# Scores leave PSUM in segments of up to 1024 keys, and outputs share one bank, in a streaming encoder layer

## The chip, the cores and the metric

The kernel runs on one core of one Trainium2 chip. The metric is device time in microseconds (us), less is better. Engines: PE is TensorE (matmul, with PEld its weight loads), DVE is VectorE, ACT is ScalarE, POOL is GpSimd, and SP issues the DMAs. PSUM is where matmuls write; the kernel divides it into eight banks, each of 512 float32 columns on 128 partitions.

## The reference

One layer of an encoder is computed for a prompt of 2048 rows and for eight sampled streams of 16 new rows with 512 cached keys. Two attention branches run side by side: differential attention (four heads, each with two softmax components) and stick-breaking attention (eight heads).

```python
s = einsum('bqhcd,bkhcd->bhcqk', q, k) * 64 ** -0.5
p = softmax(where(mask, s, -inf), axis=-1)
w = p[:, :, 0] - lam * p[:, :, 1]                       # differential attention
...
z = einsum('bqhd,bkhd->bhqk', q, k) * 64 ** -0.5
log_1m = where(mask, log_sigmoid(-z), 0.0)
log_a = log_sigmoid(z) + cumsum(log_1m, axis=3, reverse=True) - log_1m
a = where(mask, exp(log_a), 0.0)                        # stick-breaking attention
...
ya = (rms_norm(oa) * silu(za)) @ w_branch_a
yb = (ob * silu(zb)) @ w_branch_b
y = x + gate * ((sigmoid(ga) * ya + sigmoid(gb) * yb) @ w_out)
```

The outputs are the normed `y` for prompt and sample, and the new keys and values of both branches.

## The kernel before

The program has three phases. In the first the rows are normed, modulated, transposed and written to DRAM as two float16 halves; the projection of the first rows begins there. The second, where most of the time goes, runs over eight units (`u` 0 to 7). An even unit (`kind` 0) is one differential head, an odd one (`kind` 1) two stick-breaking heads. Each unit takes the sample tile and then sixteen query tiles `t` of 128 rows. The third phase does the branch and output products of all tiles and, beside them, the sample's attention over its cache.

A step of the second phase for tile `t` mixes three streams: projections of later tiles (`project`, L428 for queries, keys, values; L504 for the gates; L517 and L521 transpose queries and keys), the scores of tile `t` (`scores`, L625), and the product of weights and values (`pv`, L703) of the tile two steps before (`PV_LAG` 2).

Scores are made in chunks of up to 512 keys. `chunk` (L632) takes one bank by `bank("s")`, runs two matmuls (L639, L640: queries are split into two halves) and, on the diagonal, a third one that adds the mask (L643). `evacuate` (L549) then reads the bank. In an even unit DVE scales it into the tile `sc_p` or `sc_n` and keeps the row maximum (L558). In an odd unit ACT writes the sigmoid into `sc_p` and the sigmoid of the negated score back into the bank (both by the helper at L119), and DVE runs a product scan over that bank into `sc_n` (`stick`, L616), from the last key to the first.

Two chunks make a segment of up to 1024 keys (`SEG` is 8 blocks of 128). For a whole segment `softmax_pair` or `stick_weights` (POOL, L622) makes the weights, `turn` splits them into float16 halves (L572 on ACT, L573 on DVE) and a DMA transposes them into `wt` (L580). `pv_block` multiplies them with the values into an output tile from `bank("o")` (L696 to L698 even, L700 and L701 odd), and `natural` reads it (L675 on ACT in an even unit, L680 on ACT and L681 on DVE in an odd one).

`BANKS` (L185) shares out the eight banks: two for projections (`mm`), three for scores (`s`), one for transposes and gates (`t`), two for outputs (`o`). They lie in one pool for the whole program. In the third phase the sample takes a bank `s` for the scores against its own new keys (L761), and for each of four pairs of streams a bank `t` for the product with cached values (L803), which ACT reads at once (`ot`, L806).

The code gives the program order, by costs in `interleave`. When the program is built, a scheduler reorders each engine's instructions along a simulated timeline, and adds the waits. An engine then runs its own in that fixed order. A tile of PSUM is taken again when all that used it are done; within one tile the waits go by bank, not by column.

Of the kernel before, what the change touches and what calls it, by code (L numbers as in the profile page):

```python
# [25 lines left out]
P = 128  # L26
# [83 lines left out]
def layer_kernel(ctx: ExitStack, tc: tile.TileContext, a: dict):  # L110
# [73 lines left out]

    BANKS = {"mm": 2, "s": 3, "t": 1, "o": 2}  # L185

    def bank(tag, dt=F32):
        return ps.tile([P, 512 if dt == F32 else 1024], dt, tag=tag, name=f"ps_{tag}", bufs=BANKS[tag])

# [435 lines left out]
    def scores(U, t, jobs):  # L625

        sc, kind = U["sc"], U["kind"]
        nch = t // 4 + 1
        own = [new_job(U, t, c, t + 1) for c in range(1 + kind)]
        jobs += own  # L630

        def chunk(c, ch):  # L632
            job = own[c if kind == 1 else 0]
            seg = job["segs"][ch * 4 // SEG]
            n = 512 if ch < t // 4 else (t % 4 + 1) * P
            p = bank("s")
            qst, kk = U["q", t], U["k"][ch]
            diag = ch == t // 4
            T.matmul(p[:, 0:n], qst[:, c, :], kk[:, c, 0:n], start=True, stop=False)  # L639
            T.matmul(p[:, 0:n], qst[:, 2 + c, :], kk[:, c, 0:n], start=False, stop=not diag)  # L640
            if diag:
                m = mask_a if kind == 0 else mask_b
                T.matmul(p[:, n - m.shape[1] : n], idb, m, start=False, stop=True)  # L643
            evacuate(job, seg, c, p, ch * 512 - seg["lo"] * P, n, sc[:, 3:4], sc[:, 4:5], ch)
            if kind == 0:
                if diag and c == 1:
                    softmax_pair(job)
                return
            i = job["segs"].index(seg)
            later = job["segs"][i + 1] if i + 1 < len(job["segs"]) else None  # L650
            stick(seg, later, ch * 512 - seg["lo"] * P, n, p)
            if ch * 4 == seg["lo"]:
                if later is not None:
                    stick_weights(job, later, None)
                if i == 0:
                    stick_weights(job, seg, later)
# [8 lines left out]
        order = [(c, ch) for ch in range(nch) for c in range(2)] if kind == 0 else \  # L665
                [(c, ch) for c in range(2) for ch in reversed(range(nch))]
        return ([(0.1, silu)] if kind == 1 else []) + [(2.0 if ch < t // 4 else (t % 4 + 1) / 2, lambda c=c, ch=ch: chunk(c, ch)) for c, ch in order]

# [34 lines left out]
    def pv(job):  # L703
# [18 lines left out]
    def sample(U, dec, qpad, cs):  # L722
# [33 lines left out]
        def scores_all():  # L756
# [33 lines left out]
        def output_cached(i):  # L790

            if i == 0:
                box["ot"] = dec.tile([P, P], F32, tag="ot", name="ot")
            vs = box.pop(("v", i))
            po = bank("t")
            for b in range(2):
                cols = slice((2 * i + b) * NS, (2 * i + b + 1) * NS)
                for c, job in enumerate(box["jobs"]):
                    r = slice(c * 64, c * 64 + 64) if kind == 1 else slice(0, P)
                    n = 0  # L800
                    for vf, wf in ((0, 0), (0, 1), (1, 0)):
                        for j in range(4):
                            T.matmul(po[r, cols], vs[:, b * 4 + j, vf, r], job["segs"][0]["wt"][:, wf * 5 + j, cols], start=(n == 0), stop=(n == 11))  # L803
                            n += 1
            c = slice(i * 32, i * 32 + 32)
            S.activation(out=box["ot"][:, c], in_=po[:, c], func=AF.Identity, scale=box["f"][:, 2:3])  # L806

# [103 lines left out]
    ab = con.tile([P, 2, KT, 9], F32, name="ab")  # L911
    with tc.tile_pool(name="p0", bufs=1) as p0:
        first_x = [free.pop() for _ in range(4)]
# [159 lines left out]
        def modulated(g):  # L1073
# [5 lines left out]
            def piece(k):  # L1079
# [3 lines left out]
                hp = box["hp"]  # L1083
                pt = bank("so"[k % 2])
                for i in range(nt):
# [56 lines left out]
    scp, wtp = (c01.enter_context(tc.tile_pool(name=n, bufs=1, reuse_waits="tile")) for n in ("scp", "wtp"))  # L1142
    (gts,) = buffers_of_4k("gt", 1)
    szs = wtp.tile([P, 4, P], F32, name="szs")
    rings = [szs[:, i, :] for i in range(4)] + [gts[:, i * P : (i + 1) * P] for i in range(4, 8)]
# [15 lines left out]
    def transposed(x16, dst, half):  # L1161

        pt = bank("s", F16)
        for k in range(KT):
            T.transpose(pt[:, k * P : (k + 1) * P], x16[:, half, k * P : (k + 1) * P], id16)  # L1165
        S.copy(out=dst[:, half * KT : (half + 1) * KT, :], in_=pt.rearrange("p (k n) -> p k n", n=P))  # L1166
# [260 lines left out]
```

## Time and profile before

| what | value |
|---|---|
| median of three runs | 2345.88 us (2344.93 to 2349.84) |
| the profiled execution, its own time | 2338.96 us |
| its span, first to last instruction | 2337.1 us |
| mean granted TensorE clock | 0.965 |
| PE, DVE, ACT, POOL busy | 2121.6, 1707.5, 1663.1, 661.3 us |
| DMA | 445.35 MB, 191 GB/s mean |

The profile shows one execution. Rows by shape read: line, engine, operation, what it writes and reads with shapes, count, then busy time, mean ns of one, and the idle time of the engine just before with what ended it. A row of waits reads: who waited for whom, total us, times, longest. Matmuls are pipelined, so a busy PE is not PE at its peak.

### The profile page before, as it was taken

The page shows a single profiled execution, that of the slowest core. Times are in us where ns is not written, and L with a number is a line of the kernel's source. Part 1 is how long each engine was busy: PE and PEld are TensorE (multiplying, and loading weights), DVE is VectorE, ACT ScalarE, POOL GpSimd, SP SyncE. Part 2 cuts the span into 40 slices and gives each one's busy share as a digit, 9 for nine tenths or more (in the row PEclk, how much of TensorE's full clock was granted, in tenths as well). Part 3 has the DMA queues.
Part 4 walks back from the last instruction along what each step waited for, and adds up shares of the span by engine and source line. Part 5 has one row for each costly group of instructions (what it writes and reads, how often), then busy time and mean ns, then how long its engine had stood idle before and what let it go on. Part 6 is the DMA issues. An engine that isn't in the chain of part 4 may idle for free. (4 is left out here: it accounts for less than half of the span.)

```text
span 2337.1 us, 42708 instructions
## 1 busy us (share of the span) xinstructions
PE 2121.6 (91%) x15272; PEld 1144.0 (49%) x15272; DVE 1707.5 (73%) x3653; ACT 1663.1 (71%) x3292; POOL 661.3 (28%) x578
## 2 busy tenths in 40 slices
PE   5998898998989899899999979999995878989998
PEld 3654454545545445445545545554553444544443
DVE  4658765779875677978667797777788777777663
ACT  4968777787877778778677777866777656756541
POOL 1222022356300334731024474103345111121111
PEclk7999999999999999999999999999997988999999
DMA  9777659897895898867577777756677999999521
GB/s 333 275 214 180 152 118 272 179 193 168 212 210 126 216 204 192 179 178 192 134 191 176 185 168 186 195 146 150 146 171 166 285 254 233 257 245 236 155 98 53
DMA packets 834358, 445.35 MB, mean 191 GB/s; under 512 B 537210, under 2 KB 777130, under 8 KB 833632
## 3 DMA queue, kind: packets, MB, share of 16 engines
q1 hardware_dynamic: 833196, 442.24, 76.0%
q8 instruction: 119, 1.95, 0.4%
q14 instruction: 95, 0.78, 0.1%
q10 hardware_dynamic: 948, 0.39, 0.1%
HBM read 245.60 MB, written 69.24 MB: 135 GB/s over the span
## 5 line engine op out<-in xcount | busy, mean ns | idle before, releaser
L622 POOL TENSOR_TENSOR sc_p<-sc_p,sc_n 128x127 f32<-128x127 f32 (+7 forms) x192 | 313.8, 1638 | 826.5 <-DVE sc_n L616 812.2
L428 PE MATMUL ps_mm<-wb,hs 128*128 128x512 f16 x1632 | 414.5, 382 | 1.5 <-DMA hs<-hT_d 1.3
L428 PEld LDWEIGHTS <-hs 128*128 128x128 f16 x3120 | 274.4, 98 | 257.3 <-DMA hs<-hT_d 11.8
L428 PE MATMUL ps_mm<-wa,hs 128*128 128x512 f16 x1488 | 374.6, 382 | 9.8 <-DVE qbuf L463 6.4
L616 DVE TENSOR_TENSOR_SCAN sc_n<-ps_s,sc_n,zero_t 128x512 f32<-128x512 f32 x192 | 245.4, 1278 | 68.4 <-ACT ps_s L119 65.0
L639 PE MATMUL ps_s<-k,qst 128*128 128x512 f16 (+3 forms) x640 | 224.2, 351 | 37.9 <-DVE sc_n L616 29.9
L573 DVE TENSOR_TENSOR sc_n<-sc_p,sc_n 128x128 f16<-128x128 f32 (+7 forms) x192 | 212.7, 1112 | 58.1 <-ACT sc_n L572 57.6
L504 PEld LDWEIGHTS <-hs 128*128 128x128 f16 x1632 | 156.6, 98 | 188.3 <-ACT qst L532 6.2
L119 ACT ACTIVATE sc_p<-ps_s,usc 128x512 f32<-128x512 f32 (+3 forms) x320 | 204.8, 640 | 30.2 <-PE ps_s L640 25.3
L640 PE MATMUL ps_s<-k,qst 128*128 128x512 f16 (+3 forms) x640 | 224.2, 352 | 0.0
L572 ACT CAST sc_n<-sc_p 128x128 f16<-128x128 f32 (+7 forms) x192 | 155.5, 813 | 78.5 <-POOL sc_p L622 76.9
L700 PE MATMUL ps_o<-v,wt 128*128 128x128 f16 x1088 | 171.5, 225 | 32.6 <-DMA wt<-sc_n 32.2
L119 ACT ACTIVATE ps_s<-ps_s,usc 128x512 f32<-128x512 f32 (+3 forms) x328 | 200.0, 610 | 0.0
L504 PE MATMUL ps_t<-wa,hs 128*128 128x512 f16 x816 | 192.9, 383 | 7.6 <-ACT qst L532 6.0
L504 PE MATMUL ps_t<-wb,hs 128*128 128x512 f16 x816 | 191.9, 380 | 1.2 <-DVE qst L532 0.8
L1344 PE MATMUL ps_o<-wo,wb 128*128 128x512 f16 x816 | 186.5, 383 | 4.1 <-ACT wb L1166 4.1
L701 PE MATMUL ps_o<-v,wt 128*128 128x64 f16 x1088 | 157.9, 197 | 0.0
L700 PEld LDWEIGHTS <-wt 128*128 128x128 f16 x1088 | 105.1, 101 | 98.1 <-DMA wt<-sc_n 45.1
L558 DVE TENSOR_SCALAR_CACHE_REDUCE sc_p<-ps_s,usc 128x512 f32<-128x512 f32 (+3 forms) x160 | 106.3, 665 | 42.4 <-PE ps_s L640 31.7
L616 DVE TENSOR_TENSOR_SCAN sc_n<-ps_s,zero_t 128x128 f32<-128x128 f32 (+3 forms) x128 | 104.1, 814 | 44.0 <-ACT ps_s L119 43.4
L558 DVE TENSOR_SCALAR_CACHE_REDUCE sc_n<-ps_s,usc 128x512 f32<-128x512 f32 (+3 forms) x160 | 106.3, 665 | 36.9 <-PE ps_s L640 26.3
L701 PEld LDWEIGHTS <-wt 128*128 128x128 f16 x1088 | 103.1, 100 | 54.3 <-issue 1.1
(360 smaller groups left out, 4493.6 us busy)
## 6 DMA issues: line engine op xcount, KB each, us to landing
hs<-hT_d SPq DMA_DIRECT2D x130, 512.0 KB, 4.2
g_d<-gt SPq DMA_DIRECT2D x68, 256.0 KB, 4.2
wb<-g_d SPq DMA_DIRECT2D x26, 512.0 KB, 4.8
out_dram<-pr SPq DMA_DIRECT2D x204, 64.0 KB, 2.3
o_d<-o SPq DMA_DIRECT2D x136, 64.0 KB, 2.2
hs<-o_d SPq DMA_DIRECT2D x17, 512.0 KB, 5.6
out_dram<-x SPq DMA_DIRECT2D x17, 512.0 KB, 2.8
wide<-in_w_ada_dram SPq DMA_DIRECT2D x8, 1024.0 KB
```

Of the source, the lines that this page charges most:

```text
L119: i = S.activation(**kw)
L428: T.matmul(box["p"], box["h"][:, hi, k, :], U["w"][k][:, wi, :], start=(n == 0), stop=(n == 3 * KT - 1))
L504: T.matmul(box["g"][:, 0:gw], box["h"][:, hi, k, :], U["wg"][k // per][:, k % per, wi, :], start=(j == 0), stop=(j == 3 * KT - 1))
L558: V.tensor_scalar(out=dst[:, lo : lo + n], in0=p[:, 0:n], scalar1=sc_pos, scalar2=None, op0=ALU.mult, op1=ALU.max, accum_out=job["mx"][:, ...
L573: V.tensor_tensor(out=lo, in0=src, in1=hi, op=ALU.subtract)
L616: V.tensor_tensor_scan(out=dst[:, lo : lo + n][:, ::-1], data0=src[:, 0:n][:, ::-1], data1=zero_t[:, 0:1].to_broadcast([P, n]), initial=fi ...
L622: G.tensor_tensor(out=p[:, 0:m], in0=p[:, 0:m], in1=n[:, 1 : m + 1], op=ALU.mult)
L639: T.matmul(p[:, 0:n], qst[:, c, :], kk[:, c, 0:n], start=True, stop=False)
L640: T.matmul(p[:, 0:n], qst[:, 2 + c, :], kk[:, c, 0:n], start=False, stop=not diag)
L700: T.matmul(po[:, c * P : (c + 1) * P], wt[:, wj, :], vt[:, c, :, :], start=first, stop=False)
L701: T.matmul(po[:, c * P : c * P + 64], wt[:, nb + wj, :], vt[:, c, 0, :], start=False, stop=last)
L1344: T.matmul(po, st["y"][:, yi * 8 + k, :], wo[j * 4 + k // 2][:, wi, k % 2, :], start=(n == 0), stop=(n == 3 * KT - 1))
```

## The change

In the second phase a score tile has two banks, and there are two such tiles (four banks in place of three). `chunk` becomes a part of a segment: the matmuls of both parts write into the two banks of one tile, and only behind the last part is the tile evacuated and scanned, in one instruction each for up to 1024 columns. A segment of up to 512 keys takes a two-bank tile as well. In an even unit both parts of a component now come before the other component. The outputs get one bank, as one tile that lives through the phase, and steps alternate between its halves. In the first phase the five banks of `s` and `o` become one ring of five. In the third phase `s` has three and `o` two again; the sample's scores against its new keys move to the bank `t`, and the four products with cached values gather in one bank, which ACT reads once.

```diff
-    BANKS = {"mm": 2, "s": 3, "t": 1, "o": 2}
+    BANKS = {"mm": 2, "s": 5, "t": 1, "o": 1}
+    phase_ps = []
+    def phase_banks(stack, name):
+        phase_ps.append(stack.enter_context(tc.tile_pool(name=name, bufs=1, space=bass.MemoryType.PSUM, reuse_waits="tile")))
     def bank(tag, dt=F32):
-        return ps.tile([P, 512 if dt == F32 else 1024], dt, tag=tag, name=f"ps_{tag}", bufs=BANKS[tag])
+        pool = phase_ps[-1] if tag in "so" else ps
+        return pool.tile([P, 512 if dt == F32 else 1024], dt, tag=tag, name=f"ps_{tag}", bufs=BANKS[tag])
+    def two_banks(dt=F32):
+        return phase_ps[-1].tile([P, 1024 if dt == F32 else 2048], dt, tag="s", name="ps_s", bufs=2)
...
-        def chunk(c, ch):
+        def chunk(c, i, at):
             job = own[c if kind == 1 else 0]
-            seg = job["segs"][ch * 4 // SEG]
+            seg = job["segs"][i]
+            if "s" not in seg:
+                seg["s"] = {}
+            if at == 0:
+                seg["s"][c] = two_banks()
+            p = seg["s"][c]
+            ch = seg["lo"] // 4 + at
             n = 512 if ch < t // 4 else (t % 4 + 1) * P
-            p = bank("s")
+            x = p[:, at * 512 : at * 512 + n]
...
-            evacuate(job, seg, c, p, ch * 512 - seg["lo"] * P, n, sc[:, 3:4], sc[:, 4:5], ch)
+            nk = (seg["hi"] - seg["lo"]) * P
+            if at * 512 + n < nk:
+                return
+            evacuate(job, seg, c, p, 0, nk, sc[:, 3:4], sc[:, 4:5], i)
...
-            stick(seg, later, ch * 512 - seg["lo"] * P, n, p)
+            stick(seg, later, 0, nk, p)
...
-                U["po", t] = bank("o")
+                out_at[0] ^= 1
+                U["po", t] = outputs_of[:, out_at[0] * 256 : out_at[0] * 256 + 256]
...
-            pn = bank("s")
+            pn = bank("t")
...
             if i == 0:
-                box["ot"] = dec.tile([P, P], F32, tag="ot", name="ot")
-            vs = box.pop(("v", i))
-            po = bank("t")
+                box["po"] = bank("t")
+            vs, po = box.pop(("v", i)), box["po"]
...
-            c = slice(i * 32, i * 32 + 32)
-            S.activation(out=box["ot"][:, c], in_=po[:, c], func=AF.Identity, scale=box["f"][:, 2:3])
+            if i == 3:
+                box["ot"] = dec.tile([P, P], F32, tag="ot", name="ot")
+                S.activation(out=box["ot"], in_=po[:, 0:P], func=AF.Identity, scale=box["f"][:, 2:3])
...
-                pt = bank("so"[k % 2])
+                pt = bank("s")
...
-        pt = bank("s", F16)
+        pt = bank("s", F16) if len(phase_ps) == 3 else two_banks(F16)[:, 0:D]
...
+        BANKS.update(s=3, o=2)
+        phase_banks(c2, "ps2")
```

The scheduler makes a new order. Three places show it. The first is DVE at the end of the last odd unit, its last query tile. Before (the scan is L616, listed as SCALAR_TENSOR_TENSOR; L573 is the second half of the split; the brackets name what an instruction waits for):

```order
L616 SCALAR_TENSOR_TENSOR sc_n<-ps_s,sc_n,zero_t 128x512 [waits DVE_49,Activation_49]
L615 COPY sc_n<-sc_n 128x1 [waits DMAHW3_49,DVE_49]
L573 TENSOR_TENSOR sc_n<-sc_p,sc_n 128x896 [waits Activation_49]
L616 SCALAR_TENSOR_TENSOR sc_n<-ps_s,sc_n,zero_t 128x512 [waits DVE_49,Activation_49] x2
L573 TENSOR_TENSOR sc_n<-sc_p,sc_n 128x1024 [waits Activation_49]
L616 SCALAR_TENSOR_TENSOR sc_n<-ps_s,zero_t 128x512 [waits DMAHW4_49,PE_49,Activation_49]
L573 TENSOR_TENSOR sc_n<-sc_p,sc_n 128x1024 [waits Activation_49]
```

The same place in the changed kernel, where L626 is the scan and L583 the split:

```order
L626 SCALAR_TENSOR_TENSOR sc_n<-ps_s,sc_n,zero_t 128x1024 [waits DVE_49,PE_49,Activation_49]
L583 TENSOR_TENSOR sc_n<-sc_p,sc_n 128x1024 [waits Activation_49]
L626 SCALAR_TENSOR_TENSOR sc_n<-ps_s,zero_t 128x1024 [waits DMAHW4_49,PE_49,Activation_49]
L583 TENSOR_TENSOR sc_n<-sc_p,sc_n 128x1024 [waits Activation_49]
L625 COPY sc_n<-sc_n 128x1 [waits DMAHW5_49,DVE_49]
```

Two scans of 512 columns have become one of 1024, and scans and splits alternate.

The second place is PE some tiles earlier, where a step's last scores meet the first value product of the next tile (`wt` are the transposed weights). Before:

```order
L639 MATMUL ps_s<-k,qst 128x512 [waits DVE_49]
L640 LDWEIGHTS qst
L640 MATMUL ps_s<-k,qst 128x512
L639 LDWEIGHTS qst
L639 MATMUL ps_s<-k,qst 128x384 [waits DVE_49]
L640 LDWEIGHTS qst
L640 MATMUL ps_s<-k,qst 128x384
L643 LDWEIGHTS idb
L643 MATMUL ps_s<-masks,idb 128x128
L700 LDWEIGHTS wt [waits DMAHW5_49]
L700 MATMUL ps_o<-v,wt 128x128
```

The changed kernel at the like place (L655, L656, L659 make the scores, L722 the product):

```order
L655 MATMUL ps_s<-k,qst 128x512 [waits DVE_49]
L656 LDWEIGHTS qst
L656 MATMUL ps_s<-k,qst 128x512
L655 LDWEIGHTS qst
L655 MATMUL ps_s<-k,qst 128x256
L656 LDWEIGHTS qst
L656 MATMUL ps_s<-k,qst 128x256
L659 LDWEIGHTS idb
L659 MATMUL ps_s<-masks,idb 128x128
L722 LDWEIGHTS wt [waits DMAHW6_49]
L722 MATMUL ps_o<-v,wt 128x128 [waits DVE_49]
```

The second part of a segment no longer waits for DVE, and the first value product now does. Over the whole order 19 matmuls of L696 to L701 wait for ACT or DVE before, and 111 of their counterparts after.

The third place is ACT in the last phase, beside the sample's products with cached values. Before:

```order
L806 ACTIVATE ot<-ps_t,dsf 128x32 [waits PE_49]
L290 ACTIVATE v16c<-dc,s_c 128x8x128 [waits DMAHW0_49]
L1166 COPY wb_1399<-ps_s 128x1024 [waits PE_49] x2
L675 ACTIVATE o<-ps_s,usc_669 128x128 [waits PE_49]
L806 ACTIVATE ot<-ps_t,dsf 128x32 [waits PE_49]
L290 ACTIVATE v16c<-dc,s_c 128x8x128 [waits DMAHW6_49]
```

The changed kernel:

```order
L300 ACTIVATE v16c<-dc,s_c 128x8x128 [waits DMAHW6_49,PE_49]
L1195 COPY wb_1407<-ps_s 128x1024 [waits PE_49] x2
L697 ACTIVATE o<-ps_s,usc_672 128x128 [waits PE_49]
L300 ACTIVATE k16c<-dc,s_c 128x16x64 [waits DMAHW7_49,DMAHW6_49]
L829 ACTIVATE ot<-ps_t,dsf 128x128 [waits PE_49]
```

Thirty-two reads of 32 columns have become eight of 128.

More of the change, by code (lines that the diff above doesn't have):

```diff
@@ L645, in chunk @@
+            last = i + 1 == len(job["segs"])
             if kind == 0:
-                if diag and c == 1:
+                if last and c == 1:
                     softmax_pair(job)
                 return
-            i = job["segs"].index(seg)
-            later = job["segs"][i + 1] if i + 1 < len(job["segs"]) else None
-            stick(seg, later, ch * 512 - seg["lo"] * P, n, p)
[L652 to L656, printed above, removed]
+            later = None if last else job["segs"][i + 1]
@@ L658, in silu @@
+            stick(seg, later, 0, nk, p)
+            if later is not None:
+                stick_weights(job, later, None)
+            if i == 0:
+                stick_weights(job, seg, later)
         def silu():
@@ L663, in silu @@
             V.tensor_tensor(out=z, in0=z, in1=sg, op=ALU.mult)
[L665 to L667 removed]
+        parts = [[(i, at) for at in range(-(-(x["hi"] - x["lo"]) // 4))] for i, x in enumerate(own[0]["segs"])]
+        if kind == 0:
+            order = [(c, *x) for part in parts for c in range(2) for x in part]
+        else:
+            order = [(c, *x) for c in range(2) for part in reversed(parts) for x in part]
+        return ([(0.1, silu)] if kind == 1 else []) + \
+            [(2.0 if 2 * i + at < t // 4 else (t % 4 + 1) / 2, lambda c=c, i=i, at=at: chunk(c, i, at)) for c, i, at in order]
     def natural(U, t, po, pool=stg):
@@ L1143, in layer_kernel @@
     (gts,) = buffers_of_4k("gt", 1)
+    phase_banks(c01, "ps1")
+    outputs_of = bank("o")
+    out_at = [0]
     szs = wtp.tile([P, 4, P], F32, name="szs")
```

11 lines of the change are left out of this document (6 added, 5 removed).

## The prediction

> **What bounds the kernel now.** I read the page first, then busy time by stretch, then TensorE's waits.
>
> ```profile
> span 2337.1 us, 42708 instructions
> PE 2121.6 (91%) x15272; PEld 1144.0 (49%) x15272; DVE 1707.5 (73%) x3653; ACT 1663.1 (71%) x3292; POOL 661.3 (28%) x578
> ```
>
> Over the whole span TensorE (PE) is the busiest, and the change takes no matmul away from it. The average hides two regimes, which the stretches show (columns: busy microseconds and instruction count of PE, PEld, DVE, ACT, POOL, then granted clock, DMA share, GB/s):
>
> ```profile
> core 0: us, PE busy (x) PEld busy (x) DVE busy (x) ACT busy (x) POOL busy (x), PEclk, DMA share, GB/s
> ...
> 500.00:560.00 60.00, 51.35 (x431) 29.35 (x430) 58.57 (x74) 49.29 (x94) 44.22 (x34) 0.97 0.87 171
> 560.00:760.00 200.00, 190.34 (x1347) 105.07 (x1345) 146.20 (x389) 154.23 (x355) 40.93 (x47) 0.99 0.74 181
> ...
> 940.00:1000.00 60.00, 51.34 (x431) 28.75 (x429) 59.52 (x103) 46.00 (x97) 38.79 (x33) 1.00 0.80 170
> 1000.00:1180.00 180.00, 173.53 (x1237) 95.92 (x1236) 128.48 (x340) 136.18 (x311) 30.88 (x38) 1.00 0.68 167
> ...
> 1360.00:1420.00 60.00, 51.16 (x414) 28.44 (x413) 58.05 (x102) 43.38 (x93) 38.65 (x33) 0.97 0.71 158
> ...
> 1720.00:1800.00 80.00, 52.56 (x453) 30.97 (x450) 71.91 (x98) 64.81 (x111) 42.15 (x25) 0.84 0.76 159
> ```
>
> In the even units (560 to 760, 1000 to 1180) PE is busy 95 to 96% of the time, VectorE (DVE) and ScalarE (ACT) 71 to 77%. At the end of each odd unit it turns over: DVE is busy 58.57, 59.52 and 58.05 us of 60 and 71.91 of 80, and PE has 9 us of every 60 to spare. So DVE bounds four stretches of 260 us together, and PE the rest. What PE waits for (total us, times, longest):
>
> ```profile
> PE ps_o L700 <- DMA wt<-sc_n: 32.2, 25, 4.8
> PE ps_s L639 <- DVE sc_n L616: 29.9, 43, 2.5
> PE ps_o L696 <- DMA wt<-sc_n: 20.4, 14, 4.2
> PE ps_t L803 <- ACT ot L806: 8.0, 6, 2.3
> PE ps_s L1165 <- DVE dsc L616: 5.5, 1, 5.5
> PE ps_s L639 <- DVE sc_p L558: 4.5, 4, 2.5
> ```
>
> Scores wait for a free PSUM tile (29.9 + 4.5 us), products with the values wait for transposed weights (32.2 + 20.4 us). The change touches both chains, and the two waits of the last phase (8.0 and 5.5 us).
>
> **What larger evictions save.** By shape (count, then busy time, mean ns of one):
>
> ```profile
> L616 DVE TENSOR_TENSOR_SCAN sc_n<-ps_s,sc_n,zero_t 128x512 f32<-128x512 f32 x192 | 245.4, 1278 | 68.4 <-ACT ps_s L119 65.0
> L616 DVE TENSOR_TENSOR_SCAN sc_n<-ps_s,zero_t 128x512 f32<-128x512 f32 x32 | 38.9, 1214 | 9.1 <-ACT ps_s L119 9.1
> L616 DVE TENSOR_TENSOR_SCAN sc_n<-ps_s,zero_t 128x128 f32<-128x128 f32 x32 | 13.1, 410 | 4.0 <-ACT ps_s L119 3.7
> L558 DVE TENSOR_SCALAR_CACHE_REDUCE sc_p<-ps_s,usc 128x512 f32<-128x512 f32 x112 | 83.5, 746 | 36.1 <-PE ps_s L640 31.7 <-PE ps_s L643 4.2
> L558 DVE TENSOR_SCALAR_CACHE_REDUCE sc_p<-ps_s,usc 128x128 f32<-128x128 f32 x16 | 5.5, 342 | 2.7 <-PE ps_s L643 2.7
> L558 DVE DVE_READ_ACCUMULATOR sc_p<-ps_s,usc 128x1 f32 x160 | 13.0, 81 | 0.0
> L119 ACT ACTIVATE sc_p<-ps_s,usc 128x512 f32<-128x512 f32 x224 | 158.0, 705 | 27.5 <-PE ps_s L640 25.3 <-PE ps_s L643 1.4
> L119 ACT ACTIVATE sc_p<-ps_s,usc 128x128 f32<-128x128 f32 x32 | 11.9, 371 | 1.2 <-PE ps_s L643 1.2
> L119 ACT ACTIVATE ps_s<-ps_s,usc 128x512 f32<-128x512 f32 x224 | 152.6, 681 | 0.0
> L119 ACT ACTIVATE ps_s<-ps_s,usc 128x128 f32<-128x128 f32 x40 | 13.9, 348 | 0.0
> L119 ACT ACTIVATE sc_p<-sc_p,nm 128x1024 f32<-128x1024 f32 x40 | 45.8, 1146 | 10.4 <-DVE nm L586 10.3
> ```
>
> No eviction of 1024 columns is in this trace, so I extend each line. Scan: (1214 - 410) / 384 = 2.09 ns a column, so 1278 + 512 x 2.09 = 2350 ns, and two of 512 less one of 1024 is 206 ns. Evacuation of an even unit: 1.05 ns a column, 1285 ns plus 81 for the accumulator; 288 ns saved. Sigmoid out of PSUM: 0.87 ns, 1150 ns (the exponential of 1024 columns, out of SBUF, took 1146), 260 ns saved; in place 0.87 ns, 1125 ns, 237 ns saved. Sixteen query tiles have 40 chunks but 24 segments, so 16 pairs merge; times two heads or components, times four units, that is 128 pairs in odd and 128 in even units. ACT saves 128 x 0.497 = 64 us, DVE 128 x 0.206 + 128 x 0.288 = 26 + 37 = 63 us, out of 1663 and 1707.
>
> Nearly all of that lies beside PE. On the path it counts where DVE is the bound: the last four steps of an odd unit merge four pairs each, and some 14 of these 16 pairs fall into each stretch: 14 x 0.206 = 2.9 us, times four 11.5. I take **-10**. Bounds: 0, if DVE idles there instead, and -63, if all of it counted.
>
> The Trainium skill (Perfetto Trace Analysis, Optimizing Scalar/DVE Operations) prices the access overhead of one instruction on PSUM at about 125 ns for DVE and 51 ns for ACT; by that the first term would be 56 x 0.125 = -7 us, an estimate. The same section advises larger operations if the engine is saturated, and smaller ones if Scalar or Vector are not saturated but cause bubbles on other engines. The first half fits the four stretches, the second, which speaks against the change, the rest of the program. It is the rival of 2383 below.
>
> **What the score tiles cost.** Three tiles of one bank become two of two banks. A full tile of an odd unit was held 0.705 + 0.681 + 1.278 = 2.66 us, and will be held 1.150 + 1.125 + 2.350 = 4.63 us, 1.97 longer; in even units 0.83 becomes 1.37 us. Tiles for the odd units fall from 320 to 192. Of the 320, 43 waited, 0.70 us each (29.9 / 43). The same share of 192 is 26; if half of the longer hold shows, 26 x (0.70 + 0.98) = 44 us, **+14**. Bounds: -30, as four banks hold more than three did and all those waits may go; +39, with the whole 1.97 in each of the 26. I take the middle: a segment of up to 512 still takes a whole tile, so only two are in flight where three were. Queued behind a waiting score matmul are PE's value products and projections.
>
> **What the shared output bank costs.** The order has 19 output matmuls that wait for ACT or DVE before, and 111 after: the first product of a step waits until the tile before has been read. The trace shows what that read takes, and a step that did not wait for it:
>
> ```profile
> 1773.31 0.26 PE L701 MATMUL ps_o<-v,wt 128*128 128x64 f16 x1
> 1773.60 0.37 ACT L680 ACTIVATE ob<-ps_o,usc 128x128 f32<-128x128 f32 x1
> 1774.13 0.22 PE L700 MATMUL ps_o<-v,wt 128*128 128x128 f16 x1
> 1776.54 0.32 DVE L681 SCALAR_TENSOR_TENSOR o<-ps_o,usc,ob 128x128 f32<-128x128 f32 x1
> ```
>
> The next step's products began at 1774.13 and the read ended at 1776.86, as L681 stood behind scans: 2.7 us that PE would now stand still. Such steps are the last three of each odd unit, 12 x 2.7 = 33 us; but there PE has slack, and the order puts other matmuls in between. I take a quarter, **+8**. Bounds: 0, and 33 plus the reads by themselves in the other 52 odd and 64 even steps (0.39 + 0.34 us and 0.36 us, rows below), 33 + 38 + 23 = 94 us.
>
> ```profile
> L680 ACT ACTIVATE ob<-ps_o,usc 128x128 f32<-128x128 f32 x64 | 24.8, 387 | 3.3 <-PE ps_o L701 3.3
> L681 DVE SCALAR_TENSOR_TENSOR o<-ps_o,usc,ob 128x128 f32<-128x128 f32 x64 | 21.5, 336 | 7.5 <-ACT ob L680 7.4
> L675 ACT ACTIVATE o<-ps_o,usc 128x128 f32<-128x128 f32 x64 | 23.3, 364 | 39.8 <-PE ps_o L698 37.2 <-DMA o_d<-o 2.5
> ```
>
> The halves are thus no double buffer. The Trainium skill (PSUM — Partial Sum Buffer, PSUM bank collisions raise a hardware error) states why a schedule must do so: two engines on one bank and quadrant collide even at disjoint columns. No run here can show such a collision.
>
> **Weights become ready later.** The last segment's chain grows by the same 1.97 us (odd) and 0.54 us (even). If each of the 25 and 14 waits for weights grew by that, it would be 25 x 1.97 + 14 x 0.54 = 57 us, the upper bound; below it may be 0 or a gain of some us, since shorter ACT and DVE queues start the chain earlier. Products run two steps behind their scores and are ordered anew, so I take **+2**.
>
> **The last phase.** One read of all four groups of cached outputs takes the place of four:
>
> ```profile
> L806 ACT ACTIVATE ot<-ps_t,dsf 128x32 f32<-128x32 f32 x32 | 9.0, 282 | 9.4 <-PE ps_t L803 9.4
> ```
>
> The 8.0 us that PE stood at L803 for that read go, and the fresh keys' scores no longer hold a bank that the transposes of L1165 wait for (5.5 us): at most -14. Against it, those scores now wait until the unit before has given up the one transposing bank: up to 8 units x (0.36 + 0.34) = +6. I take **-8**. In the first phase five banks stay five: 0, hidden or not.
>
> Sum: -10 + 14 + 8 + 2 - 8 = **+6**. The profiled execution took 2338.96 us (span 2337.1), the median of the three runs shown is 2345.88; on the median, that is **2352**, and its own range, from half of each cost to double, 2338 to 2368.
>
> **The rivals.** *DVE's relief comes through and makes no new wait.* Place: the four stretches at 97% DVE. Gains of 11.5 and 8 us stand, rings and halves cost nothing: 2345.9 - 19.5 = **2326**. For it: DVE bounds there and the order keeps scans back to back; against: 43 waits on such tiles with three in flight. It decides once the rings and the shared bank cost under 10 us together. *Longer instructions make bubbles* (the page's rule): rings at their bound, the shared bank at twice my value, 39 + 16 - 10 - 8 = +37, **2383**. For it: DVE and ACT work strictly in order and each scan now blocks 2.35 us; against: the order was made anew with that in view. *Nothing is left*: PE bounds, the waits were hidden and stay hidden, the gains too: **2346**. The change does merge the evictions and does free no output bank; that is in the order, and not in doubt.
>
> **How the numbers follow.** Chances: forecast 0.45, relief 0.33, bubbles 0.14, nothing 0.08. I call faster or slower what differs by over 0.2%, 4.7 us, about what a measurement of this kernel can tell. Of the forecast's 0.45, 0.36 is slower, 0.05 same, 0.04 faster; relief gives 0.32 faster, 0.01 same; bubbles 0.14 slower; nothing 0.06 same, 0.01 each side. Faster 0.37, same 0.12, slower 0.51. The range 2322 to 2386 takes in the relief case and most of the bubbles, and leaves out a tenth at either end.
>
> **What would show it.** Right: a scan of 1024 near 2350 ns; score waits of PE near 44 us in fewer, longer pieces; products with a new wait on L681's counterpart of some 8 us; no wait for `ot` in the last phase; DVE still near 97% at the ends of odd units. Wrong: DVE there well below 95% (the two tiles starve it, dearer), score waits below 30 us (four banks beat three, cheaper), or value products that wait over 70 us for weights.

## The result and the profile after

The changed kernel takes 2372.94 us (median of 4 runs, 2370.64 to 2378.77), the kernel before 2347.47 us in the same comparison (4 runs, 2344.93 to 2349.84): a ratio of 1.0114, 95% interval 1.0093 to 1.0136. It is slower by 25 us where 6 were forecast. The time lies inside the range 2322 to 2386 and outside the 2338 to 2368 of the forecast case; the direction is right, the size is not. The page of the changed kernel, its first lines:

```profile
span 2372.4 us, 41933 instructions
PE 2134.9 (90%) x15272; PEld 1155.2 (49%) x15272; DVE 1680.8 (71%) x3269; ACT 1621.6 (68%) x3012; POOL 647.3 (27%) x578
```

DVE has 384 instructions fewer and 26.7 us less to do, ACT 280 fewer and 41.5 us less. TensorE (PE) has the same 15272 matmuls, yet it is busy 13.3 us longer and stands still longer. The larger instructions cost what was worked out for them (groups by shape of the changed kernel; L626 is the scan, L568 the evacuation of an even unit, L119 the sigmoids):

```profile
L626 DVE TENSOR_TENSOR_SCAN sc_n<-ps_s,sc_n,zero_t 128x1024 f32<-128x1024 f32 x64 | 150.2, 2347 | 63.0 <-ACT ps_s L119 62.1
L568 DVE TENSOR_SCALAR_CACHE_REDUCE sc_p<-ps_s,usc 128x1024 f32<-128x1024 f32 x40 | 51.3, 1282 | 42.3 <-PE ps_s L656 25.8 <-PE ps_s L659 16.5
L119 ACT ACTIVATE sc_p<-ps_s,usc 128x1024 f32<-128x1024 f32 x80 | 89.2, 1115 | 42.2 <-PE ps_s L656 26.2 <-PE ps_s L659 11.9 <-PE ps_o L723 3.9
L119 ACT ACTIVATE ps_s<-ps_s,usc 128x1024 f32<-128x1024 f32 x80 | 86.9, 1086 | 0.0
```

So the loss is not in the work of DVE and ACT. What PE waits for in the changed kernel (total us, times, longest; L655 is the score matmul, L718 and L722 the value products, L438 the projection, L514 the gates, L527 the key transposes, L825 the last phase):

```profile
PE ps_mm L438 <- DMA hs<-hT_d: 31.5, 20, 3.4
PE ps_s L655 <- DVE sc_n L626: 24.8, 20, 3.9
PE ps_o L722 <- DMA wt<-sc_n: 19.1, 9, 5.9
PE ps_o L722 <- DVE o L703: 14.2, 6, 7.1
PE ps_o L718 <- DMA wt<-sc_n: 13.9, 10, 5.2
PE ps_t L825 <- DMA dwt<-dsc: 12.9, 5, 5.9
PE ps_t L527 <- ACT qst L542: 11.4, 4, 5.6
PE ps_t L527 <- DVE k L305: 10.0, 7, 2.9
PE ps_t L527 <- ACT gt L517: 9.5, 14, 1.4
PE ps_t L514 <- DVE qst L542: 9.1, 8, 2.1
PE ps_s L655 <- DVE sc_n L568: 6.0, 6, 1.6
PE ps_t L825 <- DVE v16c L305: 4.6, 4, 2.8
```

The row for the input rows in the kernel before:

```profile
PE ps_mm L428 <- DMA hs<-hT_d: 2.6, 2, 1.3
```

The score waits and the waits for weights, on which the prediction dwelt, both fell (29.9 to 24.8, 52.6 to 33.0 us). Three rows are new or grew: the projections wait 31.5 us for their own input rows (2.6 before), the products 14.2 us for the read of the output tile before, and the matmuls of transposes and gates (L514, L527) 41 us where it was 28 (L504, L517), some 10 of it each time for their own input `k` and the rest for their bank. By where the last value product of the second phase ends, this phase grew by 36 us, and the last phase is shorter by 1 us, in these two executions.

How the rows come late can be read from the timeline of the changed kernel, near the end of the third odd unit (start, duration, engine, line, what; in brackets the idle time before and what ended it):

```profile
1272.96 3.65 SPq L590 DMA_TRANSPOSE wt<-sc_n  x2
...
1275.21 1.03 PE L514 MATMUL ps_t<-wa,hs 128*128 128x512 f16 x4
...
1276.70 0.53 SPq L415 DMA_DIRECT2D hs<-hT_d  x1
...
1278.16 0.27 PE L527 MATMUL ps_t<-id,k 128*128 128x128 f16 x2 [0.34 <-ACT gt L517]
...
1280.92 0.60 PE L438 MATMUL ps_mm<-wa,hs 128*128 128x512 f16 x2 [2.26 <-DMA hs<-hT_d]
```

The rows lie in three buffers, taken in turn. Gate matmuls read the same rows as the projection of their step, and run long after it: those at 1275.21 are the last of a step whose projection began at 1232.6, three steps before the one that is being fetched. Only when they are done is its buffer free: the fetch goes out at 1276.70, behind two transposing DMAs, and its projection stands until 1280.92. Counted over the 56 fetches of the odd units that reuse a buffer of the same unit, 20 had under 5.5 us from their issue to their projection, 6 before the change. The last gate matmul of a step began 18.6 us behind the last projection matmul of that step before the change (mean of 68), and 23.0 us after it.

### The profile page after: what moved, and what is told of

Its sections match the earlier page's. It is cut to its first block, busy times and chain, and to the rows that moved or that the text cites. A ratio compares the mean times of both kernels' runs of the same rounds, so it can differ in the third digit from the quotient of the medians.

```text
span 2372.4 us, 41933 instructions
## 1 busy us (share of the span) xinstructions
PE 2134.9 (90%) x15272; PEld 1155.2 (49%) x15272; DVE 1680.8 (71%) x3269; ACT 1621.6 (68%) x3012; POOL 647.3 (27%) x578
## 5 line engine op out<-in xcount | busy, mean ns | idle before, releaser
L438 PEld LDWEIGHTS <-hs 128*128 128x128 f16 x3120 | 289.9, 99 | 340.4 <-DMA hs<-hT_d 38.4
L438 PE MATMUL ps_mm<-wb,hs 128*128 128x512 f16 x1632 | 397.0, 385 | 11.7 <-DMA hs<-hT_d 11.7
L438 PE MATMUL ps_mm<-wa,hs 128*128 128x512 f16 x1488 | 359.3, 385 | 19.8 <-DMA hs<-hT_d 19.8
L655 PE MATMUL ps_s<-k,qst 128*128 128x512 f16 (+3 forms) x640 | 225.2, 353 | 34.3 <-DVE sc_n L626 24.8
L583 DVE TENSOR_TENSOR sc_n<-sc_p,sc_n 128x128 f16<-128x128 f32 (+7 forms) x192 | 212.5, 1117 | 58.3 <-ACT sc_n L582 57.6
L514 PEld LDWEIGHTS <-hs 128*128 128x128 f16 x1632 | 154.6, 99 | 184.0 <-DVE qst L542 11.0
L626 DVE TENSOR_TENSOR_SCAN sc_n<-ps_s,zero_t 128x256 f32<-128x256 f32 (+7 forms) x128 | 172.1, 1347 | 94.4 <-ACT ps_s L119 87.3
L656 PE MATMUL ps_s<-k,qst 128*128 128x512 f16 (+3 forms) x640 | 222.9, 353 | 0.0
L119 ACT ACTIVATE sc_p<-ps_s,usc 128x128 f32<-128x128 f32 (+7 forms) x192 | 166.5, 867 | 65.5 <-PE ps_s L659 34.9
L514 PE MATMUL ps_t<-wb,hs 128*128 128x512 f16 x816 | 195.9, 381 | 6.4 <-DVE qst L542 5.7
L514 PE MATMUL ps_t<-wa,hs 128*128 128x512 f16 x816 | 195.9, 383 | 3.4 <-DVE qst L542 3.4
L626 DVE TENSOR_TENSOR_SCAN sc_n<-ps_s,sc_n,zero_t 128x1024 f32<-128x1024 f32 x64 | 150.2, 2347 | 63.0 <-ACT ps_s L119 62.1
L722 PE MATMUL ps_o<-v,wt 128*128 128x128 f16 x1088 | 148.5, 228 | 33.6 <-DMA wt<-sc_n 19.1
L119 ACT ACTIVATE ps_s<-ps_s,usc 128x128 f32<-128x128 f32 (+7 forms) x192 | 161.7, 842 | 0.0
L723 PE MATMUL ps_o<-v,wt 128*128 128x64 f16 x1088 | 139.3, 200 | 0.0
L722 PEld LDWEIGHTS <-wt 128*128 128x128 f16 x1088 | 106.1, 103 | 57.3 <-DMA wt<-sc_n 25.0
L568 DVE TENSOR_SCALAR_CACHE_REDUCE sc_p<-ps_s,usc 128x1024 f32<-128x1024 f32 (+4 forms) x96 | 92.8, 967 | 54.9 <-PE ps_s L659 28.9
L1375 PEld LDWEIGHTS <-wb 128*128 128x128 f16 x816 | 78.7, 98 | 95.5 <-issue 4.4
```

What stands on the lines that cost most here:

```text
L119: i = S.activation(**kw)
L438: T.matmul(box["p"], box["h"][:, hi, k, :], U["w"][k][:, wi, :], start=(n == 0), stop=(n == 3 * KT - 1))
L514: T.matmul(box["g"][:, 0:gw], box["h"][:, hi, k, :], U["wg"][k // per][:, k % per, wi, :], start=(j == 0), stop=(j == 3 * KT - 1))
L583: V.tensor_tensor(out=lo, in0=src, in1=hi, op=ALU.subtract)
L626: V.tensor_tensor_scan(out=dst[:, lo : lo + n][:, ::-1], data0=src[:, 0:n][:, ::-1], data1=zero_t[:, 0:1].to_broadcast([P, n]), initial=fi ...
L655: T.matmul(x, qst[:, c, :], kk[:, c, 0:n], start=True, stop=False)
```

## The experiments

Each line is a median, with its ratio to the kernel before in the same comparison.

| | kernel | us | ratio, 95% interval |
|---|---|---|---|
| e1 | changed, rows fetched two steps ahead | 2387.36 | 1.0173 (1.0149 to 1.0197) |
| e2 | before, rows two ahead | 2354.98 | 1.0032 (1.0017 to 1.0046) |
| e3 | before, outputs in halves of one bank | 2380.14 | 1.0129 (1.0108 to 1.0151) |
| e4 | changed, four tiles of one bank, chunks of 512 | 2365.45 | 1.0070 (1.0051 to 1.0089) |
| e5 | changed, four row buffers | 2392.54 | 1.0201 (1.0181 to 1.0222) |
| e6 | before, four row buffers | 2347.29 | 1.0003 (0.9988 to 1.0018) |
| e7 | e3, four row buffers | 2347.68 | 1.0001 (0.9987 to 1.0015) |
| e8 | before, last phase's layout as changed | 2350.89 | 1.0021 (1.0007 to 1.0034) |
| e9 | e5, each half evacuated when it is made | 2570.29 | 1.0939 (1.0921 to 1.0957) |
| e10 | e4, four row buffers | 2362.83 | 1.0060 (1.0046 to 1.0074) |
| e11 | changed, instructions of 512 columns | 2411.63 | 1.0261 (1.0232 to 1.0290) |
| e12 | e7, two banks for transposes and gates | 2319.20 | 0.9864 (0.9839 to 0.9888) |

**e1 and e2, rows fetched two steps ahead.**

```diff
-            if i == H_AT and not at_hand and m + 1 < len(steps) and steps[m + 1] not in ahead:
-                fetch_h(*steps[m + 1])
+            if i == H_AT and not at_hand:
+                for k in (m + 1, m + 2):
+                    if k < len(steps) and steps[k] not in ahead:
+                        fetch_h(*steps[k])
```

> The changed kernel, and the rows of a projection (hs) are fetched two steps ahead instead of one; nothing else. Theory A (rows come late): in the changed kernel PE waited 31.5 us at L438 for hs, because the fetch stands on SP's queue behind transposing DMAs that wait for DVE, and the loss of 25 us is mostly this. Then the wait falls below 5 us and the time to 2343 to 2353. Rival B (the wait only moves): PE was ahead of DVE anyway, so the time it wins at L438 is lost at the score tiles (L655) or at the transposed weights (L718, L722): hs wait gone, the other waits up by 20 us or more, time 2365 to 2376.

> Control: the kernel before with the same earlier fetch of the rows. Its own wait at L428 for hs is below 3 us. Theory A: within 4 us of the kernel before (2343 to 2351). Rival C (an earlier fetch helps any version, by taking SP's queue out of the way): 2330 to 2342, and then e1 says nothing on the change.

Neither theory was met: the wait for rows stayed (32.6 us), and the kernel lost 14 us more. The experiment did not do what it was meant to: the fetches went out as late as before (17 of the 56 with under 5.5 us to spare), since a fetch one step earlier needs a buffer that is given up one step earlier, and the late gates hold it. This is what pointed to the buffers. e2 moved by 7 us although its rows had not been late; edits that should do nothing move the time of this kernel by up to that, as the order of all engines is made anew. Differences below some 8 us between two builds are therefore not read as causes here.

**e3, the shared output bank alone.**

```diff
-                U["po", t] = bank("o")
+                out_at[0] ^= 1
+                U["po", t] = outputs_of[:, out_at[0] * 256 : out_at[0] * 256 + 256]
```

> The kernel before, and only the outputs of the second phase share one bank in halves (its second output bank stays empty there); scores by chunks of 512 in three banks, last phase as before. The prediction's term was +8 us. In the changed kernel PE waited 14.2 us at L722 for L703. If that adds up: 2355 to 2362. Rival: PE has slack there, within 3 us of before. Rival D (the shared bank is most of the loss): 2365 or more.

Rival D: 33 us, more than the whole loss of the change (25 us), with three score tiles and chunks of 512 as before. The waits of PE in e3:

```profile
PE ps_mm L428 <- DMA hs<-hT_d: 24.8, 10, 4.4
PE ps_s L639 <- DVE sc_n L616: 23.5, 27, 3.0
PE ps_o L700 <- DMA wt<-sc_n: 20.3, 15, 5.0
PE ps_o L700 <- DVE o L681: 17.6, 6, 8.3
```

The products wait 17.6 us for the bank, as could be foreseen. The late rows are there too, with nothing else changed: the gates lag 22.4 us behind their projections. In the profiled executions the second phase is 29 us longer than before and the last phase, which the edit does not touch, 12 us.

**e4, four tiles of one bank in the changed kernel.** `two_banks()` becomes a bank per chunk, with four of them in the second phase, and each chunk is evacuated and scanned at once.

> The changed kernel with chunks of 512 again, evacuated and scanned one by one, in a ring of four tiles of one bank; halves of the output bank and the last phase as changed. If the long instructions or the two-bank tiles make the rows late (by DVE's longer chain ahead of the transposing DMAs): hs wait below 10 us, time 2340 to 2355. If the shared output bank or the new order as such does it: hs wait above 20 us, time 2362 to 2376.

Neither case in full: the hs wait (12.6 us) is near the first, the time in the second. The kernel is 15 us faster than e3, and 7 faster than the changed one.

**e5, e6 and e7, a fourth row buffer.** The last of eight weight buffers serves as the fourth, and is given back for the last phase.

```diff
-        ahead[u, t] = hs[len(fetched) % 3].bitcast(F16)...
+        h_ring.append(h_ring.pop(0))
+        ahead[u, t] = h_ring[-1].bitcast(F16)...
...
+    wb7 = wb8.pop()
+    h_ring.insert(0, wb7)
```

> The changed kernel with four buffers for the rows of a projection in place of three (the fourth is the last of the eight weight buffers wb, given back before the last phase). Theory A2 (row buffers): in e1 the fetch two ahead did not start earlier, since the buffer that it needs is held by the gate matmuls (L514) of three steps before; these ended at 1243.0, 1260.5, 1275.9 us, and the fetches were issued at 1243.5, 1260.9, 1276.7. With a fourth buffer the hs wait at L438 falls from 31.5 us below 8 and the time from 2373 to 2340 to 2358. Rival B (the wait only moves, to score tiles, gates or transposed weights): hs wait below 8, time 2365 to 2380.

> Control: the kernel before with the same fourth row buffer. Its hs wait is 2.6 us; theory A2: within 7 us of before (2340 to 2354; an edit that moved hardly anything, e2, moved the time by 7). Rival C (row buffers bound any version): 2325 to 2338.

> e3 (only the shared output bank, 2380 us) with four row buffers. If the shared bank costs what it costs by late gates, so that rows come late (24.8 us of hs wait in e3), 2345 to 2360. If it costs by its own waits (17.6 us at L700 for L681) and by what these set back, 2368 to 2384.

With a fourth row buffer the 33 us of e3 are gone (2380.14 to 2347.68), while the same buffer gives the kernel before nothing (e6). PE's waits for rows in e7 are down to 1.0 us, listed under the name of the fourth buffer, `wb`, and the direct wait for the bank is still there:

```profile
PE ps_s L641 <- DVE sc_n L618: 32.6, 31, 4.2
PE ps_o L698 <- DMA wt<-sc_n: 20.9, 17, 3.0
PE ps_o L702 <- DMA wt<-sc_n: 20.4, 17, 3.6
PE ps_s L641 <- DVE sc_n L560: 15.0, 10, 3.5
PE ps_o L702 <- DVE o L683: 13.4, 6, 7.1
PE ps_mm L430 <- DMA wb<-hT_d: 1.0, 1, 1.0
```

The gates are as late as in e3 (23.4 us behind their projections), but no fetch has to wait for them: all 56 go out before the gates of three steps back have ended. So a bank that is waited for, and gates that are late, cost little once the rows no longer hang on them. That the late rows cost all of the 33 is not shown. In the profiled executions the second phase, where the rows are fetched, is 12 us shorter in e7 than in e3, and the last phase 14; its length differs by nearly as much between kernels that have the same code there (532.3 us before, 544.8 in e2).

In the changed kernel the same cure does not work: e5 is slower by 20 us, which is rival B, past its bound of 2380. Its waits:

```profile
PE ps_s L657 <- DVE sc_n L628: 37.9, 25, 4.5
PE ps_o L724 <- DMA wt<-sc_n: 25.7, 16, 3.4
PE ps_t L827 <- DMA dwt<-dsc: 23.3, 8, 9.3
PE ps_t L529 <- ACT gt L519: 22.0, 6, 6.5
PE ps_o L720 <- DMA wt<-sc_n: 14.2, 14, 4.4
PE ps_s L657 <- DVE sc_p L570: 13.3, 11, 4.4
PE ps_s L657 <- DVE sc_n L570: 7.1, 5, 3.1
```

The wait for rows is gone as well (1.8 us), but score tiles (the three rows of L657 make 58 us, in the changed kernel 34), transposed weights (40 against 33) and, in the last phase, the sample's weights (L827, 23.3 against 12.9) took more than it gave. The read of the gates grew too (22.0 against 9.5), but transposes and gates together stand at 41 us in both.

**e8, the last phase alone** (the three hunks of the diff on `pn`, `po` and `ot`, applied to the kernel before).

> The kernel before, and only the sample's layout as changed (its new keys' scores in the bank t, one read for four groups of cached outputs). The prediction's term was -8 us, at most -14, and up to +6 against it: 2333 to 2345. Rival: the last phase moves by 12 us between builds of the same code anyway (532.5 us before, 545.1 in e2), so 2340 to 2358 with no wait for ot.

The rival: 4 us slower (1.6 to 8.0), in a program whose last phase moves by that anyway. The products wait for `ot` no more, but for other things (`dwt` 13.5 us against 9.5, `v16c` 7.2 against 0.5), and the transposes behind the one read wait 5.0 us for it.

**e9, each half of a two-bank tile by itself.** Half of a tile is evacuated and scanned as soon as it is made, the later half first.

> e5 (changed kernel, four row buffers, 2392 us), with each half of a two-bank tile evacuated and scanned by itself as soon as it is made; the tile is still given back as a whole. The hs wait stays near nothing. Theory L (the long instructions make the bubbles: a scan cannot start until a whole segment is made and through ACT; DVE waits for ACT at the scan 149 us in the changed kernel against 108 before): DVE's wait there back below 125 us, time 2345 to 2365. Rival G (the grain of the ring: two tiles in flight, also for a segment of up to 512 keys): score waits at L655 stay above 35 us, time 2378 to 2395.

This did not separate the two theories; the time is far past both. The second half's matmul belongs to a tile whose first half is being read, and it waits for the tile: 595 of the 640 score groups wait for DVE in its order, 322 in the changed kernel, and 253 of the 256 second halves wait for DVE on their own tile. So in a tile of two banks a wait goes by the tile, and not by bank as said of tiles ahead of the prediction. PE's waits at the scores:

```profile
PE ps_s L657 <- DVE sc_n L628: 110.4, 80, 4.2
```

It shows that in this program a two-bank tile is better filled before it is read, and says nothing on the long instructions.

**e10, e4 with four row buffers.**

> e4 (changed kernel with four tiles of one bank and chunks of 512, 2365 us) with four row buffers. Its hs wait was 12.6 us. Theory L and rival G both expect 2335 to 2352 (e7, with three such tiles, gave 2348; the fourth tile and the last phase are worth up to 14 us). If it stays at 2362 or above, the new last phase or the order as such costs, and the tiles are not the cause.

The third case: the wait for rows is gone (12.6 us to 1.0), yet the kernel is no better than e4 by more than builds differ, and 15 us over e7, though its scores have a bank more. It differs from e7 also by the new last phase, by the order of chunks in even units and by the one ring of the first phase; of these only the last phase was priced (e8, 4 us).

**e11, the changed kernel with instructions of 512 columns.** Both halves are made first, then each is evacuated and scanned by its own instructions.

```diff
-            evacuate(job, seg, c, p, 0, nk, sc[:, 3:4], sc[:, 4:5], i)
+            cuts = [(x, min(x + 512, nk)) for x in range(0, nk, 512)][::-1 if kind else 1]
+            for lo, hi in cuts:
+                evacuate(job, seg, c, p[:, lo:hi], lo, hi - lo, sc[:, 3:4], sc[:, 4:5], 2 * i + lo // 512)
...
-            stick(seg, later, 0, nk, p)
+            for lo, hi in cuts:
+                stick(seg, later, lo, hi - lo, p[:, lo:hi])
```

> The changed kernel (three row buffers), only that a segment of over 512 keys, once both its halves are made, is evacuated and scanned by two instructions of up to 512 columns each; unlike e9, no matmul stands between the two. Tiles, halves of the output bank and last phase as changed. Theory L (long instructions): DVE's wait for ACT at the scan falls from 149 us below 125, time 2345 to 2362. Rival G (ring and order): 2366 to 2382 with PE's waits much as in the changed kernel. Theory S (the merge itself saves, as the prediction's -10 has it): 2380 to 2390.

Theory S, and beyond its bound: undoing the merge costs 39 us more (2411.63 against 2372.94). In tiles of two banks the merge gains. It does not pay for such tiles, though: four tiles of one bank with chunks of 512 (e4, 2365.45) are no slower than two of two banks with the merge. DVE waits less for ACT at the scan, as theory L had it (123.2 us against 149.4), and that did not help: the second row is the split behind the scan (57.6 us in the changed kernel).

```profile
DVE sc_n L626 <- ACT ps_s L119: 123.2, 72, 8.2
DVE sc_n L583 <- ACT sc_n L582: 83.0, 78, 4.6
```

What the merge gives shows in PE's waits of e11:

```profile
PE ps_s L655 <- DVE sc_n L626: 36.3, 24, 4.7
PE ps_o L725 <- DMA wt<-sc_n: 31.5, 22, 4.8
PE ps_o L721 <- DMA wt<-sc_n: 17.8, 13, 2.5
PE ps_s L655 <- DVE sc_p L568: 13.3, 10, 4.0
PE ps_s L655 <- DVE sc_n L568: 10.0, 8, 2.8
```

PE waits 60 us for score tiles, 34 with the merge, and 49 us for weights, 33 with it. The trace shows why for the tiles: from ACT's first read to the end of the last scan a tile of 1024 keys of an odd unit is held 6.35 us in halves and 4.83 us merged (means of 80), as a tile goes back only when both halves are done.

**e12, a second bank for transposes and gates.** e7 leaves one bank empty in the second phase; `t` takes it there (`BANKS.update(s=3, t=2)`, its pool made anew for each phase; in the first phase scores and outputs share a ring of five as in the change).

> e7 (outputs in halves of one bank, four row buffers, chunks of 512 in three tiles of one bank, old last phase; 2348 us) with the bank that it leaves empty given to transposes and gates (t) in the second phase. Before, PE waited some 26 us at L504 and L517 for t, and late gates hold the row buffers. Theory T: gates end sooner, those waits go, 2322 to 2340. Rival: PE's win is lost at score tiles and transposed weights, 2343 to 2360.

Theory T, a little past its bound: 2319.20 us, 1.4% (1.1 to 1.6) faster than the kernel before, the fastest of all. Gates (L516) no longer wait for `t`, and the key transposes (L529) for nothing over 0.6 us but their own input (`k`, 13.3 us).

The gates now lag 8.0 us behind their projections (18.6 before, 23.4 in e7), and the mean time from a row's fetch to its projection is 41 us where it was 26 in e7 and 13 before. The time that was won does not show at transposes and gates, though: the 15 us for their bank in e7 are gone, but they now wait 25 us for their inputs, so that all their waits are as long as in e7 (24 and 25 us). Less is waited for score tiles (52 us in e7, 41 here) and for transposed weights (41 and 26). Why these fell was not tried.

## Why the prediction was right in direction and wrong in size

The parts of the change, taken in one order, add up: outputs in halves alone, +32.6 us (e3); on top of it the two-bank tiles with what goes with them (last phase, order of even units, one ring in the first phase), still with instructions of 512, +30 (e11 at +62.7); on top of that the merge, -37 (the changed kernel at +25.5). In another order the shares would differ, as e7 and e5 show. The end of the last value product parts the profiled executions (one of each kernel, up to 9 us off its median) into phases:

| | second phase ends at, us | last phase, us |
|---|---|---|
| before | 1804.9 | 532.3 |
| e3 | 1834.1 | 544.7 |
| e11 | 1884.7 | 531.7 |
| changed | 1841.1 | 531.3 |
| e7 | 1822.5 | 530.6 |
| e12 | 1782.1 | 541.1 |

So in the second phase alone the three steps are some +29, +51 and -44. The forecast had +8, +14 and -10 for them: every sign right, every size some two to four times too small. That the sum still fell inside the range is in part luck, as the errors of two costs and one gain offset each other.

- *Larger evictions, -10.* The durations are right: 2347 against 2350 ns for the scan, 1282 against 1285, 1115 against 1150, 1086 against 1125. By durations the saving on DVE is right too: the scans' groups of the second phase fell from 349.5 to 322.3 us, the evacuations' from 212.6 to 185.6, the accumulator reads' by 10 us, 64 in all where 63 were forecast. But the records of neighbours on an engine overlap (DVE's durations before add up to 1917.8 us, its busy time is 1707.5), and busy time fell by 26.7 us on DVE and 41.5 on ACT, where 63 and 64 were set against it. The share on the path was mis-sized: -37, not -10, inside the bound of -63. I counted only DVE's relief in four stretches, 11.5 us together. What I left out is that the merge gives a two-bank tile back sooner (4.83 us in place of 6.35, e11), and that PE then waits 26 us less for score tiles and 16 less for weights.
- *Score tiles, +14.* The mechanism is right, the size too small: from e3 to e11 PE's waits for score tiles doubled, from 30 to 60 us (44 were forecast, from 30), with +30 in the medians and +51 in the second phase, the latter above the bound of +39. In the changed kernel this cannot be seen, since the merge takes it back: the three rows of L655 quoted or named above make 33.5 us (24.8, 6.0 and 2.7), and the first has 20 pieces where 26 were forecast.
- *Shared output bank, +8.* This is the step that failed. "I take a quarter" priced the standing of PE at the bank, and that wait did come: 14.2 us in 6 pieces on the read of the output tile, where some 8 were named. What was not in the sum is what else stands behind that wait on PE: gates, whose end frees the row buffers, and with them the next fetch. e3 measured +33, with waits for rows of 24.8 us where they were 2.6, and with a fourth row buffer (e7) both are gone; how much of the 33 the late rows are stays open, as said there. The queue behind a waiting score matmul was named in the prediction, and that behind a waiting value product was not; SP's queue of fetches was not looked at. In the trace of before a fetch already went out within 1 us of the gates' end in 27 of 56 cases.
- *Weights later, +2.* The waits for weights fell by 19.6 us instead (52.6 to 33.0). They fell as much with the shared bank alone (34.0 in e3), stood at 49.3 with two-bank tiles read in halves (e11), and fell again with the merge. Why was not tried.
- *Last phase, -8.* The gain did not come: +4 in e8, less than builds differ by, so that not even its sign is shown. In the changed kernel the two waits that I wanted gone fell (8.0 us to none, 5.5 to 2.0), and others grew on the same chain (`dwt` 9.5 to 12.9, `v16c` 0.5 to 4.6).
- *The range of the forecast case, 2338 to 2368.* It does not follow from its own terms: with the gains as they stand, half of each cost gives -6 us and double +30, so 2340 to 2376 on the median. The measured 2372.94 lies outside the one and inside the other.
- *DVE at the ends of the odd units.* It was to stay near 97%; the four stretches before make 95% together, and only three of them 97 or more. In the changed kernel these stretches, which come 5 to 35 us later, read:

```profile
505.00:565.00 60.00, 54.24 (x455) 30.79 (x454) 54.80 (x56) 50.41 (x78) 42.63 (x33) 1.00 0.90 187
955.00:1015.00 60.00, 49.09 (x421) 28.84 (x422) 53.80 (x77) 45.96 (x78) 39.97 (x34) 0.94 0.99 192
1383.00:1443.00 60.00, 53.01 (x440) 30.16 (x439) 58.91 (x88) 43.07 (x79) 41.68 (x33) 0.97 0.82 177
1755.00:1835.00 80.00, 50.70 (x441) 32.42 (x438) 73.55 (x81) 61.48 (x81) 45.23 (x26) 0.81 0.71 152
```

  DVE is busy 91, 90, 98 and 92% (98, 99, 97 and 90% before): starved a little in two of the four, with more waiting for ACT's sigmoids at the scan (149.4 us against 108.4 over the program). So two of the signs of being wrong came, and they were to point opposite ways: DVE below 95% (dearer) and score waits below 30 us (24.8, cheaper). The first pointed the right way.

The rival of 2383 (bubbles) came nearer in time than the forecast, but not by its mechanism. Its rule, smaller operations where Scalar or Vector are not saturated but cause bubbles on other engines (the Trainium skill, Perfetto Trace Analysis, Optimizing Scalar/DVE Operations), speaks against the merge. Here the measurement decides against the rule for tiles that go back as a whole: with smaller operations in the same tiles e11 was slower by 39 us. Where the tile is as small as the operation, smaller ones were not slower (e4). That relief makes no new wait (2326) fell with the wait for rows.

What stays open: why the fourth row buffer, which cures e3, makes the changed kernel slower (e5) and does nothing for e4 (e10). The late rows of the changed kernel are thus not shown to be what makes it slower. The waits of e5 say where the time went, and no run says whether the ring of two tiles or the order made anew sends it there.

## What to carry to other kernels

When a bank is taken away from a consumer, price not only its own wait but what is queued behind it on the same engine and which buffers those instructions hold: here the gates, and not only the products, stood behind it, and they set when the next rows could be fetched. A small ring that is refilled just in time (here three row buffers, fetched within 1 us of their release in half of the cases) is where such a delay shows, and a buffer more is a cheap test of it; it can also only move the wait, as in e5. A larger tile has a price that larger instructions on it may just pay back: price both together, against small tiles in as many banks (e4). A bank that is freed is worth trying at a stage whose lateness holds others up: the one that the output halves free gained 28 us over e7 once transposes and gates had it.

## What the hardware showed beside

Short waits can cost TensorE twice: the granted clock falls to half around or behind some of them. These are stretches of the changed kernel around the wait that ended at 1280.92 (the column before the last two is the clock), and PE's projections right behind it:

```profile
1270.00:1280.00 10.00, 8.31 (x67) 4.51 (x65) 4.74 (x8) 5.61 (x13) 0.60 (x3) 1.00 0.79 175
...
1282.00:1286.00 4.00, 4.00 (x12) 1.51 (x11) 1.92 (x4) 1.60 (x3) 0.74 (x2) 0.57 0.08 20
1286.00:1290.00 4.00, 4.00 (x22) 1.90 (x20) 0.31 (x1) 2.44 (x4) 0.00 (x0) 1.00 0.78 148
```

```profile
1280.92 1.54 PE L438 MATMUL ps_mm<-wa,hs 128*128 128x512 f16 x6 [2.26 <-DMA hs<-hT_d]
1282.24 4.42 PE L438 MATMUL ps_mm<-wb,hs 128*128 128x512 f16 x12
```

Six projections take 1.54 us, and the twelve that follow 4.42. Seven of the 22 stretches at half clock between 100 and 1900 us begin within 2.5 us before or behind the end of a wait for rows of 2.0 to 3.4 us; most of the others lie beside waits for something else. Together the stretches make 126 us in the changed kernel and 79 us before, and with them go the mean clock, 0.958 against 0.965, and the 13.3 us by which PE is busy longer with the same matmuls. The Trainium skill (TensorE: Matmul & The Clock Gate, What's actually happening) has half rate as the state after at least one idle window of about 3.4 us; here six of these seven waits were shorter by themselves than that (2.26 us in the rows above).
